# Overlapping the up-projection units of a gated feed-forward block by half, and taking their follow-up work one by one from a list

## The chip, the cores and the metric

The kernel runs on one core of a Trainium2 chip. The metric is device microseconds of one execution, the median of several runs. The core's engines run their own queues in order: TensorE (PE, with its weight loads as PEld), VectorE (DVE), ScalarE (ACT), GpSimd (POOL) and SyncE (SP), which here only issues transfers.

## What is computed

One layer of a streaming encoder over 2048 positions of width 1024: a mixer (pooling and a gated recurrence) and then the part that this change touches, a feed-forward block with a short convolution over the positions.

```python
def conv_glu_ffn(x, w_up, conv_w, conv_b, w_down):
    S = x.shape[1]
    h = x @ w_up                                   # 1024 -> 2 * 2816
    hp = jnp.pad(h, ((0, 0), (CONV_WIDTH - 1, 0), (0, 0)))
    hc = sum(conv_w[j] * hp[:, j:j + S] for j in range(CONV_WIDTH)) + conv_b
    val, gate = jnp.split(hc, 2, axis=-1)
    return (jax.nn.silu(gate) * val) @ w_down
...
        x = x + conv_glu_ffn(rmsnorm(x, norm2_g[l]), w_up[l], conv_w[l], conv_b[l], w_down[l])
```

All values are float32. D_FF is 2816, which is 22 tiles of 128.

## The kernel before, in words

The positions are worked off in two rounds of 1024, each round as two halves of 512 (hf 0 and 1): mixer, output projections, up-projection, down-projection. `ffn` (from line 1327) does the last two.

A **unit** m of the up-projection (m = 0 to 21) makes four results of 128 channels by 512 positions: the value and the gate (s = 0 and 1) of channel tile m, for both halves. It does so with seven products instead of eight (a Winograd scheme of 2 by 2 blocks, the blocks being the two halves of the 1024 inputs, value and gate, and the two halves of the positions). A product is a sum over four tiles of inputs, and since each float32 operand is split into a high and a low part, each tile takes three matmuls: twelve matmuls of 128 by 128 by 512 per product (`Unit.multiply`, line 146 being the helper's line for every matmul). The combinations of the positions ("forms", 56 tiles) are made once per round and stay in place; those of the weights are read from memory as raw tiles.

The products are added up in three PSUM banks per unit: P1 and P2 in X, P6, P7 and P4 in Z, P5 and P3 in V. Between them copies are taken (`Unit.after`): e1 is X after P1 (ScalarE, line 993), u2 is e1 - Z after P6 (VectorE, line 995), u3 is Z - e1 after P7 (line 999). P7 must wait for u2, since it adds to the bank that u2 reads; P4 must wait for u3, and P3 for the result h of the gate's second half (line 959), which reads V. The order within a unit is P1, P6, P5, P7, P2, P4, P3. P2 completes the value of half 0, P7 the gate of half 1, P4 the gate of half 0 (line 957), P3 the value of half 1.

The order of the units (`up_order`): units 0 and 1 alternate, then 2 and 3 (their first two products ahead of the rest), and from unit 4 on one unit follows the other whole.

What follows a result (`emit_up`): `conv` copies two halo columns (GpSimd, lines 1343 and 1345), takes the first tap on ScalarE (line 1348) and adds two taps on VectorE (lines 1350 and 1352); `glu` takes SiLU on ScalarE (line 1356) and multiplies gate and value on VectorE (lines 1358 and 1360; GpSimd does line 1360 for units 0 to 3). `add_forms` then makes the seven operands of the down-projection from the gated tiles of two neighbouring units: three are the tiles themselves, stored by SP (line 1334), and four are sums on GpSimd (line 1065), stored from its queue (line 1372). The down-projection (`Rows`, tiles dn_P) fetches them back (line 777) and splits them (lines 578 and 579).

Weights come as a stream: SP loads raw tiles (line 183, eight buffers), ScalarE makes the high part (line 205) and VectorE the low part (line 206) of an operand tile `ops`, of which there are six. So the cast for product j waits until product j - 6 has been done. Casts are placed at most four products ahead of the product that is being written.

The rest of the working tiles share one pool of 77 slots, of which the forms hold 56 during the up-projection. A new tile waits until its slot's last user is done, the store of a form among them.

The order on each engine comes from a scheduler that plays the program with durations of its own and puts instructions where they could start; a program line says what depends on what. `behind` forces one instruction behind another on the same engine, `in_turn` keeps an instruction from being placed ahead of the last matmul written so far. Neither makes a semaphore. In `ffn` the convolutions and gates of a result are written where the result is, all that are due at once; the sums of forms are written two products after their gate (`later`, `turn`, `FORM_LAG`), and the stores at the next product that is not P3 (`flush`).

Of the kernel before, what the change touches and what calls it, by code (L numbers as in the profile page):

```python
# [14 lines left out]
AF = mybir.ActivationFunctionType  # L15
ALU = mybir.AluOpType
# [11 lines left out]
MF = D_FF // P  # L28
EPS = 1e-6
TB = 512  # L30
# [19 lines left out]
ORDER = ("P1", "P6", "P5", "P7", "P2", "P4", "P3")  # L50
# [11 lines left out]
N_HEADS = 2  # L62
# [7 lines left out]
N_RAW = 8  # L70
GROUP = 4
SUM_LAG = 7
FORM_LAG = 2
N_OPS = 6
LOOKAHEAD = 4
MM_PER_TICK = 6
# [3 lines left out]
def tile_trunk(  # L80
# [16 lines left out]
    pe, act, dve, pool, sp = nc.tensor, nc.scalar, nc.vector, nc.gpsimd, nc.sync  # L97
# [9 lines left out]
    def slot(name, cols=TB, dt=F32):  # L107
        return slots.tile([P, cols], dt, tag="s", name=name, padded_shape=[P, 528])
# [121 lines left out]
    def behind(ins, other):  # L230

        tc.add_manual_dep(ins.ins, other.ins.name, mybir.DependencyInfo(
            mybir.DependencyClass.NoSync, mybir.DependencyReason.DATA), reason="behind")

    def in_turn(ins):

        tc.add_manual_dep(ins.ins, count[1].ins.name, mybir.DependencyInfo(
            mybir.DependencyClass.NoSync, mybir.DependencyReason.SCHED_ONLY), reason="in turn")
# [159 lines left out]
    def up_order():  # L398
        heads = [(0, 1), (2, 3), (4, 5)][:N_HEADS]
        res = [(m, p) for ms in heads for p in ("P1", "P2") for m in ms]  # L400
        res += [(m, p) for ms in heads for p in ("P6", "P5", "P7", "P4", "P3") for m in ms]
        return res + [(m, p) for m in range(2 * N_HEADS, MF) for p in ORDER]

    def plan_ffn():
        units = {}
        for m, p in up_order():
            if m not in units:
                units[m] = sums_of_unit(w_up_t, m, MF + m, sums["up"], m)
            fn, raws = units[m][p]()
            stream.op("up", fn, raws)  # L410
        plan_rows("dn", w_dn, R_DN, MF // 2)
# [91 lines left out]
    o_n1, o_n2, o_bg, o_ps, o_lb, o_hg, o_cb, o_cw = offs  # L503
# [8 lines left out]
    def col(o):  # L512
        return cols[:, o : o + 1]
# [97 lines left out]
    def norm_rows(src, name, xs, after, lag=1):  # L611
        for j in range(NT):
            while (src, j) not in ready:
                yield 1
            halves = [xt[src, j, c] for c in range(2)]
            t = [slot(f"{name}xs{j}_{hf}") for hf in range(2)]
            r = row_rstd(halves, t, f"{name}{j}")
            if lag:
                yield lag
            for hf in range(2):  # L620
                dve.tensor_scalar(t[hf], halves[hf], r[:, 0:1], None, ALU.mult)
                xs[j, hf] = t[hf]
            after(j)
# [327 lines left out]
    def value(dst, a, ps):  # L951
        if a is None:
            act.copy(dst, ps)
            return
        t, how = a
        if how == "from":
            dve.tensor_tensor(dst, ps, t, ALU.subtract)  # L957
        else:
            dve.tensor_tensor(dst, t, ps, ALU.add if how == "add" else ALU.subtract)  # L959

    class Unit:
# [28 lines left out]
        def after(self, p):  # L990
            bk, t = self.bank, self.t
            if p == "P1":
                act.copy(self.tmp("e1"), bk["X"])
            elif p == "P6":
                dve.tensor_tensor(self.tmp("u2"), t["e1"], bk["Z"], ALU.subtract)  # L995
            elif p == "P2":
                self.emit(0, 0, None, bk["X"])
            elif p == "P7":
                dve.tensor_tensor(self.tmp("u3"), bk["Z"], t["e1"], ALU.subtract)  # L999
                self.emit(1, 1, (t["u3"], "add"), bk["V"])  # L1000
            elif p == "P4":
                self.emit(1, 0, (t["e1"], "from"), bk["Z"])
            elif p == "P3":
                self.emit(0, 1, (t["u2"], "sub"), bk["V"])
# [54 lines left out]
    def add_forms(two, forms, k, name, store=lambda p, t: None, sums=True, pin=lambda i: None):  # L1059

        def comb(p, x0, x1, op):
            if (p, k) in forms or x0 is None or x1 is None:
                return
            t = slot(f"{name}_{p}_{k}")
            pin(pool.tensor_tensor(t, x0, x1, op))  # L1065
# [12 lines left out]
        comb("P3", forms.get(("P6", k)), two.get((1, 1)), ALU.add)  # L1078
# [247 lines left out]

    def ffn(b0, forms, late):
        gd, gt, gp = {}, {}, {}
        later, turn = [], [0]
        stores = []  # L1330

        def flush():
            for d, g in stores:
                sp.dma_start(d, g)
            stores.clear()

        def emit_up(m):
            hs, ts = {}, {}

            def conv(s, hf):  # L1340
                mt = m + MF * s
                h = hs[s, hf]
                pool.tensor_copy(h[:, 0:2], hist[:, mt] if hf == 0 else hs[s, 0][:, TB : TB + 2])  # L1343
                if hf == 1:
                    pool.tensor_copy(hist[:, mt], h[:, TB : TB + 2])  # L1345
                t = slot(f"e{b0}_{m}_{s}_{hf}")
                ts[s, hf] = t
                act.activation(t, h[:, 2:], AF.Identity, bias=col(o_cb + mt),  # L1348
                               scale=col(o_cw + 4 * MF + mt))
                dve.scalar_tensor_tensor(t, h[:, 1 : 1 + TB], col(o_cw + 2 * MF + mt), t,  # L1350
                                         ALU.mult, ALU.add)
                dve.scalar_tensor_tensor(t, h[:, 0:TB], col(o_cw + mt), t, ALU.mult, ALU.add)  # L1352

            def glu(hf):
                g = ts[1, hf]
                act.activation(g, g, AF.Silu)  # L1356
                if hf:
                    dve.scalar_tensor_tensor(g, g, -1.0, ts[0, hf], ALU.mult, ALU.mult)  # L1358
                else:
                    (pool if m < G_POOL else dve).tensor_tensor(g, g, ts[0, hf], ALU.mult)  # L1360
                k = m // 2
                two = gp.setdefault(k, {})
                two[hf, m % 2] = g

                def store(p, t):
                    name = f"dg{b0}_{p}_{k}"
                    d = dram.tile([P, TB], F32, tag=name, name=name)
                    gd[p, k] = d
                    if p in R_FORM:
                        stores.append((d, t))  # L1370
                    else:
                        pool.dma_start(d, t)  # L1372

                have = dict(two)
                add_forms(have, gt, k, f"gf{b0}", store, False)
                later.append((turn[0] + FORM_LAG, lambda: add_forms(
                    have, gt, k, f"gf{b0}", store, True, in_turn)))

            def emit(s, hf, a, ps):
                h = slot(f"h{b0}_{m}_{s}_{hf}", 2 + TB)  # L1380
                hs[s, hf] = h
                value(h[:, 2:], a, ps)
                first = (0, 0) if m >= 2 * N_HEADS else (1, 0)
                if (s, hf) == first:
                    conv(0, 0)
                if (s, hf) == (1, 0):
                    conv(1, 0)
                    glu(0)
                elif (s, hf) == (0, 1):
                    conv(0, 1)  # L1390
                    conv(1, 1)
                    glu(1)

            return emit

# [40 lines left out]
        for n, (m, p) in enumerate(up_order()):  # L1436
            if n == GO_AT:
                go_up[0] = True
            if m not in units:
                units[m] = Unit(f"up{b0}_{m}", "up", emit_up(m))  # L1440
            u = units[m]
            u.multiply(p, forms, late)
            turn[0] = n
            while later and later[0][0] <= n:
                later.pop(0)[1]()
            if p != "P3":
                flush()
            u.after(p)
            if m == MF - 1 and p in EARLY:
                down.make(EARLY[p])  # L1450

        for _, fn in later:
            fn()
        last = b0 + 2 >= SEQ // TB
        nxt = []

# [104 lines left out]
```

## Time and profile before

| | us |
|---|---|
| runs of the kernel | 2723.14, 2713.98, 2723.79 (median 2723.14) |
| the profiled execution | 2727.51, its span 2725.0 |
| mean granted TensorE clock of its span | 0.977 of full speed |
| up-projection, first round | 689.0 to 1165.4 |
| up-projection, second round | 2017.1 to 2495.7 |

Times in the profile count from the first instruction. Tile names are printed without numbers: up_X, up_Z and up_V are the three banks, up_e, up_u (both u2 and u3) and h the copies, e the convolved and gated tiles, gf_P the sums and dg_P their copies in memory, ops the weights' operand tiles, raw the loaded weights. The forms show the product in a matmul's name: m_f0 to m_f3 is P1, m_f4 to m_f7 P2, m_T1 P5, m_T2 P6, m_T3 P7, m_T4 P4, m_B22 P3; the letter h or l is the high or low part. In a row of the timeline stand start, duration, engine, line, operation, tiles, and in brackets the idle time before it and what ended that.

### The profile page before, as it was taken

The numbers are of one execution on the slowest core, as the hardware profiler recorded it, in microseconds if no ns is written. First come the engines' busy times: TensorE is split into PE (matmuls) and PEld (weight loads), VectorE is DVE, ScalarE is ACT, GpSimd is POOL, SyncE is SP. The second block draws the span as 40 slices with busy tenths as digits, with TensorE's granted clock in tenths as the row PEclk, the third lists the DMA queues.
The fourth block names the chain that finished last, engine by engine and source line by source line (L and its number), as shares of the span: only waits on it lengthen the run. The fifth ranks groups of instructions, "written<-read, shape, count | busy, mean of one in ns | idle before, by whom it ended". The sixth has DMA issues, their size and how long they took to land. (4 is left out here: it accounts for less than half of the span.)

```text
span 2725.0 us, 35432 instructions
## 1 busy us (share of the span) xinstructions
PE 2568.9 (94%) x11464; PEld 2077.4 (76%) x11464; DVE 1990.4 (73%) x3390; ACT 1166.1 (43%) x2204; POOL 963.7 (35%) x1273
## 2 busy tenths in 40 slices
PE   7899999889989999989989999999998899999998
PEld 6678887767767777768868788888786677777886
DVE  7888878358787777766577787675779777777744
ACT  5333434214544444444464344442355444444533
POOL 5544343061453343443253111201434323324402
PEclk8999999989989999999999999999999999999999
DMA  5656567889577788899888434346343443435942
GB/s 204 214 147 167 169 160 196 247 256 250 159 191 207 206 225 234 239 315 352 246 243 236 132 120 132 120 154 231 121 151 105 132 127 131 144 125 190 342 143 105
DMA packets 258313, 515.75 MB, mean 189 GB/s; under 512 B 26224, under 2 KB 42736, under 8 KB 257648
## 3 DMA queue, kind: packets, MB, share of 16 engines
q1 hardware_dynamic: 177600, 301.01, 34.1%
q0 software_dynamic: 51040, 129.52, 19.6%
q10 hardware_dynamic: 29488, 82.96, 8.6%
q8 instruction: 90, 1.47, 0.2%
q14 instruction: 95, 0.78, 0.1%
HBM read 422.69 MB, written 206.05 MB: 231 GB/s over the span
## 5 line engine op out<-in xcount | busy, mean ns | idle before, releaser
L205 ACT CAST ops<-raw 128x512 fp32r<-128x512 f32 x732 | 451.2, 620 | 932.6 <-PE up_Z L146 241.5
L206 DVE TENSOR_TENSOR ops<-raw,ops 128x512 fp32r<-128x512 f32 x732 | 563.4, 773 | 300.7 <-ACT ops L205 292.5
L1348 ACT ACTIVATE e<-h,cols 128x512 f32<-128x512 f32 x176 | 138.6, 813 | 19.3 <-DVE h L959 8.6
L1352 DVE SCALAR_TENSOR_TENSOR e<-h,cols,e 128x512 f32<-128x512 f32 x176 | 144.3, 825 | 0.0
L1065 POOL TENSOR_TENSOR gf_P<-e,e 128x512 f32<-128x512 f32 x44 | 77.8, 1769 | 171.8 <-DVE e L1358 113.0
L1350 DVE SCALAR_TENSOR_TENSOR e<-h,cols,e 128x512 f32<-128x512 f32 x176 | 134.6, 787 | 3.4
L777 POOL DMA_DIRECT2D g_P<-dg_P x154 | 86.2, 565 | 135.4 <-PE dn_P L146 49.5
L1343 POOL COPY h<-h 128x2 f32<-128x2 f32 x88 | 54.2, 642 | 152.8 <-DVE h L957 152.8
L1345 POOL COPY hist<-h 128x2 f32<-128x2 f32 x88 | 40.7, 462 | 180.3 <-DVE h L959 180.0
L146 PE MATMUL up_Z<-m_T30h,ops 128*128 128x512 f32 x88 | 39.6, 450 | 53.8 <-DVE up_u L995 53.8
L1276 POOL TENSOR_TENSOR ya<-ya,gl 128x512 f32<-128x512 f32 x32 | 46.2, 1473 | 112.0 <-DVE gl L1268 110.5
L999 DVE TENSOR_TENSOR up_u<-up_Z,up_e 128x512 f32<-128x512 f32 x44 | 30.4, 690 | 72.5 <-PE up_Z L146 72.4
L146 PEld LDWEIGHTS up_Z<-m_T30h,ops 128*128 128x128 f32 x88 | 17.2, 195 | 71.4 <-DVE up_u L995 38.1
L826 POOL COPY qm<-q 128x64 f32<-128x64 f32 x64 | 28.9, 462 | 118.2 <-DVE q L850 25.0
L1356 ACT ACTIVATE e<-e 128x512 f32<-128x512 f32 x88 | 54.9, 624 | 32.9 <-DVE e L1352 32.8
L1209 ACT ACTIVATE gt<-gt,cols 128x512 f32<-128x512 f32 x48 | 34.8, 725 | 78.8 <-DVE gt L959 61.3
L1172 POOL TENSOR_TENSOR q<-q,qs 128x512 f32<-128x512 f32 x16 | 21.9, 1371 | 127.4 <-ACT qs L1171 114.3
L1041 DVE TENSOR_TENSOR ac<-ac,dn_P 128x512 f32<-128x512 f32 x72 | 46.8, 682 | 27.7 <-PE dn_P L146 20.2
L959 DVE TENSOR_TENSOR h<-up_u,up_V 128x512 f32<-128x512 f32 x88 | 60.2, 684 | 5.4 <-PE up_V L146 3.9
L1065 POOL TENSOR_TENSOR gf_P<-gf_P,e 128x512 f32<-128x512 f32 x44 | 59.0, 1340 | 11.0 <-DVE e L1358 10.3
L1372 POOL DMA_DIRECT2D dg_P<-gf_P x88 | 55.6, 632 | 19.3 <-POOL gf_P L1065 18.7
L1041 DVE TENSOR_TENSOR x<-x,wo_P 128x512 f32<-128x512 f32 x88 | 56.1, 680 | 7.7 <-PE wo_P L146 7.6
(1270 smaller groups left out, 8367.7 us busy)
## 6 DMA issues: line engine op xcount, KB each, us to landing
g_P<-dg_P POOLq DMA_DIRECT2D x154, 256.0 KB, 7.1
raw<-in_w_up_t SPq DMA_DIRECT2D x132, 256.0 KB, 2.9
raw<-in_w_in_t SPq DMA_DIRECT2D x98, 256.0 KB, 2.9
dg_P<-gf_P POOLq DMA_DIRECT2D x88, 256.0 KB, 3.4
raw<-in_w_io SPq DMA_DIRECT2D x68, 256.0 KB, 5.2
dg_P<-e SPq DMA_DIRECT2D x66, 256.0 KB, 3.0
raw<-in_w_dn SPq DMA_DIRECT2D x66, 256.0 KB, 6.0
x<-in_x SPq DMA_DIRECT2D x64, 256.0 KB, 5.2
```

The costliest lines, as they stand in the source:

```text
L146: count[1] = pe.matmul(*args, **kw)
L205: self.mark = act.copy(hi, v)
L206: dve.tensor_tensor(lo, v, f32(hi), ALU.subtract)
L777: eng.dma_start(t, d)
L959: dve.tensor_tensor(dst, t, ps, ALU.add if how == "add" else ALU.subtract)
L1041: dve.tensor_tensor(t, t, ps[j], ALU.add if sg > 0 else ALU.subtract)
L1065: pin(pool.tensor_tensor(t, x0, x1, op))
L1348: act.activation(t, h[:, 2:], AF.Identity, bias=col(o_cb + mt), scale=col(o_cw + 4 * MF + mt))
L1350: dve.scalar_tensor_tensor(t, h[:, 1 : 1 + TB], col(o_cw + 2 * MF + mt), t, ALU.mult, ALU.add)
L1352: dve.scalar_tensor_tensor(t, h[:, 0:TB], col(o_cw + mt), t, ALU.mult, ALU.add)
L1356: act.activation(g, g, AF.Silu)
L1372: pool.dma_start(d, t)
```

## The change

From unit 4 on the products of unit m are given the places 7m, 7m + 2, ... 7m + 12, and sorted. So two neighbouring units alternate, half a unit apart: P7 of unit m, P1 of m+1, P2 of m, P6 of m+1, P4 of m, P5 of m+1, P3 of m, P7 of m+1, and so on.

The convolutions, gates and sums of forms are no longer written where the result is, but put on a list, `work`; after each product one entry of it is written (`drain(1)`; sums of forms cost nothing and are written as soon as they stand first). A unit adds six entries and has seven products, and units 0 to 3 add six each too, mostly at once. The taps on ScalarE and SiLU are kept `in_turn`, and the first VectorE tap of a convolution is also put `behind` the newest u2 or u3. What was still on the list is written after the last product. The stores are issued after every product, P3 as well. The number of instructions does not change.

```diff
-        return res + [(m, p) for m in range(2 * N_HEADS, MF) for p in ORDER]
+
+        rest = [(7 * m + 2 * i, m, p) for m in range(2 * N_HEADS, MF)
+                for i, p in enumerate(ORDER)]
+        return res + [(m, p) for _, m, p in sorted(rest)]
...
+    def first(ins):
+
+        urgent[0] = ins
+
+    def second(ins):
+        if urgent[0] is not None:
+            behind(ins, urgent[0])
+        return ins
...
-                dve.tensor_tensor(self.tmp("u2"), t["e1"], bk["Z"], ALU.subtract)
+                first(dve.tensor_tensor(self.tmp("u2"), t["e1"], bk["Z"], ALU.subtract))
...
-                dve.tensor_tensor(self.tmp("u3"), bk["Z"], t["e1"], ALU.subtract)
+                first(dve.tensor_tensor(self.tmp("u3"), bk["Z"], t["e1"], ALU.subtract))
...
+        def drain(n):
+            while work and (n or not work[0][0]):
+                k, fn = work.pop(0)
+                n -= k
+                fn()
...
-                act.activation(t, h[:, 2:], AF.Identity, bias=col(o_cb + mt),
-                               scale=col(o_cw + 4 * MF + mt))
-                dve.scalar_tensor_tensor(t, h[:, 1 : 1 + TB], col(o_cw + 2 * MF + mt), t,
-                                         ALU.mult, ALU.add)
+                in_turn(act.activation(t, h[:, 2:], AF.Identity, bias=col(o_cb + mt),
+                                       scale=col(o_cw + 4 * MF + mt)))
+                in_turn(second(dve.scalar_tensor_tensor(t, h[:, 1 : 1 + TB],
+                                                        col(o_cw + 2 * MF + mt), t,
+                                                        ALU.mult, ALU.add)))
...
-                act.activation(g, g, AF.Silu)
+                in_turn(act.activation(g, g, AF.Silu))
...
-                later.append((turn[0] + FORM_LAG, lambda: add_forms(
-                    have, gt, k, f"gf{b0}", store, True, in_turn)))
+                work.append((0, lambda: add_forms(have, gt, k, f"gf{b0}", store, True, in_turn)))
...
                 if (s, hf) == first:
-                    conv(0, 0)
+                    work.append((1, lambda: conv(0, 0)))
                 if (s, hf) == (1, 0):
-                    conv(1, 0)
-                    glu(0)
+                    work.append((1, lambda: conv(1, 0)))
+                    work.append((1, lambda: glu(0)))
                 elif (s, hf) == (0, 1):
-                    conv(0, 1)
-                    conv(1, 1)
-                    glu(1)
+                    work.append((1, lambda: conv(0, 1)))
+                    work.append((1, lambda: conv(1, 1)))
+                    work.append((1, lambda: glu(1)))
...
             u.multiply(p, forms, late)
-            turn[0] = n
-            while later and later[0][0] <= n:
-                later.pop(0)[1]()
-            if p != "P3":
-                flush()
+            flush()
             u.after(p)
+            drain(1)
...
-        for _, fn in later:
-            fn()
+        while work:
+            drain(1)
```

What it moves is shown by the orders of the two programs. First VectorE where units follow one another: the twelve rows around u2 of unit 9 in the first round. In `up0_9_u2` the 0 is the round and 9 the unit; in `e0_8_0_1` stand round, unit, s and half; ops and raw carry the number of the product. Before:

```order
L206 TENSOR_TENSOR ops239_8206<-raw225_8009,ops239_8206 128x512
L1350 SCALAR_TENSOR_TENSOR e0_8_0_1_8165<-h0_8_0_1_8161,cols_84,e0_8_0_1_8165 128x512
L1350 SCALAR_TENSOR_TENSOR e0_8_1_1_8171<-h0_8_1_1_8091,cols_84,e0_8_1_1_8171 128x512
L1352 SCALAR_TENSOR_TENSOR e0_8_0_1_8165<-h0_8_0_1_8161,cols_84,e0_8_0_1_8165 128x512
L1360 TENSOR_TENSOR e0_8_1_0_8137<-e0_8_1_0_8137,e0_8_0_0_8113 128x512
L1352 SCALAR_TENSOR_TENSOR e0_8_1_1_8171<-h0_8_1_1_8091,cols_84,e0_8_1_1_8171 128x512
L206 TENSOR_TENSOR ops240_8230<-raw226_8039,ops240_8230 128x512
L206 TENSOR_TENSOR ops241_8247<-raw227_8063,ops241_8247 128x512
L1358 SCALAR_TENSOR_TENSOR e0_8_1_1_8171<-e0_8_1_1_8171,e0_8_0_1_8165 128x512
L995 TENSOR_TENSOR up0_9_u2_8221<-up0_9_e1_8197,up0_9_Z_8199 128x512
L206 TENSOR_TENSOR ops242_8273<-raw228_8080,ops242_8273 128x512
L999 TENSOR_TENSOR up0_9_u3_8263<-up0_9_Z_8199,up0_9_e1_8197 128x512
```

Now (the line numbers are those of the changed program, u2 being line 1008, u3 1012, the taps 1369 and 1372, the gate 1378, the cast 205):

```order
L1012 TENSOR_TENSOR up0_8_u3_8061<-up0_8_Z_7944,up0_8_e1_7911 128x512
L205 TENSOR_TENSOR ops236_8103<-raw222_7903,ops236_8103 128x512
L972 TENSOR_TENSOR h0_8_1_1_8063<-up0_8_u3_8061,up0_8_V_7997 128x512
L1369 SCALAR_TENSOR_TENSOR e0_7_0_1_8067<-h0_7_0_1_8037,cols_84,e0_7_0_1_8067 128x512
L1372 SCALAR_TENSOR_TENSOR e0_7_0_1_8067<-h0_7_0_1_8037,cols_84,e0_7_0_1_8067 128x512
L1369 SCALAR_TENSOR_TENSOR e0_7_1_1_8093<-h0_7_1_1_7885,cols_84,e0_7_1_1_8093 128x512
L205 TENSOR_TENSOR ops237_8134<-raw223_7928,ops237_8134 128x512
L1372 SCALAR_TENSOR_TENSOR e0_7_1_1_8093<-h0_7_1_1_7885,cols_84,e0_7_1_1_8093 128x512
L205 TENSOR_TENSOR ops238_8164<-raw224_7954,ops238_8164 128x512
L1378 SCALAR_TENSOR_TENSOR e0_7_1_1_8093<-e0_7_1_1_8093,e0_7_0_1_8067 128x512
L1008 TENSOR_TENSOR up0_9_u2_8147<-up0_9_e1_8089,up0_9_Z_8127 128x512
L205 TENSOR_TENSOR ops239_8189<-raw225_7977,ops239_8189 128x512
```

u2 of unit 9 stood behind cast 241 and the gate of unit 8, with two casts and two convolutions of unit 8 close before it; it now stands behind cast 238 and the gate of unit 7. Its P6 is product 235 before and 233 now.

Second, VectorE around u2 of unit 4, the first that used to run alone. Before:

```order
L206 TENSOR_TENSOR ops206_7377<-raw192_7149,ops206_7377 128x512
L1350 SCALAR_TENSOR_TENSOR e0_3_0_1_7285<-h0_3_0_1_7281,cols_84,e0_3_0_1_7285 128x512
L1350 SCALAR_TENSOR_TENSOR e0_3_1_1_7291<-h0_3_1_1_7159,cols_84,e0_3_1_1_7291 128x512
L1352 SCALAR_TENSOR_TENSOR e0_3_0_1_7285<-h0_3_0_1_7281,cols_84,e0_3_0_1_7285 128x512
L1352 SCALAR_TENSOR_TENSOR e0_3_1_1_7291<-h0_3_1_1_7159,cols_84,e0_3_1_1_7291 128x512
L206 TENSOR_TENSOR ops207_7399<-raw193_7170,ops207_7399 128x512
L1358 SCALAR_TENSOR_TENSOR e0_3_1_1_7291<-e0_3_1_1_7291,e0_3_0_1_7285 128x512
L995 TENSOR_TENSOR up0_4_u2_7351<-up0_4_e1_7327,up0_4_Z_7329 128x512
L999 TENSOR_TENSOR up0_4_u3_7389<-up0_4_Z_7329,up0_4_e1_7327 128x512
```

Now:

```order
L205 TENSOR_TENSOR ops204_7274<-raw190_7069,ops204_7274 128x512
L1369 SCALAR_TENSOR_TENSOR e0_2_1_0_7241<-h0_2_1_0_7153,cols_84,e0_2_1_0_7241 128x512
L1372 SCALAR_TENSOR_TENSOR e0_2_1_0_7241<-h0_2_1_0_7153,cols_84,e0_2_1_0_7241 128x512
L205 TENSOR_TENSOR ops205_7299<-raw191_7092,ops205_7299 128x512
L1008 TENSOR_TENSOR up0_4_u2_7285<-up0_4_e1_7263,up0_4_Z_7267 128x512
L205 TENSOR_TENSOR ops206_7321<-raw192_7116,ops206_7321 128x512
L1369 SCALAR_TENSOR_TENSOR e0_3_0_0_7288<-h0_3_0_0_6693,cols_84,e0_3_0_0_7288 128x512
L1369 SCALAR_TENSOR_TENSOR e0_3_1_0_7311<-h0_3_1_0_7178,cols_84,e0_3_1_0_7311 128x512
L1372 SCALAR_TENSOR_TENSOR e0_3_0_0_7288<-h0_3_0_0_6693,cols_84,e0_3_0_0_7288 128x512
```

Before, all convolutions and gates of units 2 and 3 stood ahead of it. Now the second half of unit 2 and all of unit 3 follow it: it is row 1080 of VectorE's order and was row 1096.

More of the change, by code (lines that the diff above doesn't have):

```diff
@@ L72 @@
 SUM_LAG = 7
-FORM_LAG = 2
 N_OPS = 6
@@ L233, in behind @@
             mybir.DependencyClass.NoSync, mybir.DependencyReason.DATA), reason="behind")
+    urgent = [None]
+    def first(ins):
[4 more added lines that the diff above has]
+        return ins
     def in_turn(ins):
@@ L1328, in ffn @@
         gd, gt, gp = {}, {}, {}
-        later, turn = [], [0]
+        work = []
         stores = []
```

## The prediction

> **What bounds the kernel now.** I read the busy shares first, then the list of who waited for whom on TensorE, then windows around the two up-projection stages, then the timeline of TensorE, VectorE and GpSimd inside a stage. The page's first part says who is full, and the waits say what little stops it (columns: total us, times, longest).
>
> ```profile
> PE 2568.9 (94%) x11464; PEld 2077.4 (76%) x11464; DVE 1990.4 (73%) x3390; ACT 1166.1 (43%) x2204; POOL 963.7 (35%) x1273
> ```
> ```profile
> PE up_Z L146 <- DVE up_u L995: 53.8, 20, 8.3
> PE x_t L627 <- DVE x_xs L621: 10.1, 4, 7.7
> PE dn_P L146 <- ACT dn_P_10h L578: 7.4, 1, 7.4
> ```
>
> TensorE is busy for 94% of the span, and no other engine is near that. The one wait of size is in the stage that the change touches: 53.8 us in 20 pieces, each time a product into bank Z waiting for VectorE's `up_u`, the copy (u2) that must be taken out of Z before the next product is added to it. The windows give the two rounds, each split into units 0 to 3 and units 4 to 21 (first column after the stretch: its length; then busy us of PE, PEld, DVE, ACT, POOL, clock, DMA share, GB/s).
>
> ```profile
> 689.00:783.30 94.30, 86.83 (x369) 67.92 (x368) 78.61 (x109) 49.44 (x87) 45.33 (x52) 0.96 0.65 171
> 783.30:1165.40 382.10, 358.95 (x1514) 285.74 (x1514) 290.53 (x403) 173.43 (x275) 148.22 (x209) 0.98 0.80 223
> 2017.00:2111.10 94.10, 86.78 (x370) 67.91 (x369) 79.67 (x109) 49.56 (x88) 39.88 (x48) 0.96 0.34 107
> 2111.10:2495.70 384.60, 359.90 (x1514) 286.79 (x1514) 292.58 (x403) 172.81 (x276) 127.10 (x191) 0.98 0.42 136
> ```
>
> The timeline of TensorE gives the price of one product of twelve matmuls, and shows the hole.
>
> ```profile
> 874.63 0.40 PE L146 MATMUL up_V<-m_B223h,ops 128*128 128x512 f32 x1
> 877.41 0.39 PE L146 MATMUL up_X<-m_f3h,ops 128*128 128x512 f32 x1
> 880.20 0.40 PE L146 MATMUL up_Z<-m_T23h,ops 128*128 128x512 f32 x1
> ...
> 882.99 0.39 PE L146 MATMUL up_V<-m_T13h,ops 128*128 128x512 f32 x1
> 885.42 0.50 PE L146 MATMUL up_Z<-m_T30h,ops 128*128 128x512 f32 x1 [2.05 <-DVE up_u L995]
> ```
> ```profile
> 904.79 0.39 PE L146 MATMUL up_V<-m_T13h,ops 128*128 128x512 f32 x1
> 905.20 0.47 PE L146 MATMUL up_Z<-m_T30h,ops 128*128 128x512 f32 x1
> ```
>
> The first three rows are the last matmuls of P3, P1 and P6: 874.63, 877.41, 880.20, so 2.78 us a product without a wait. P5 ends with the row at 882.99; P7 should start 0.23 us later and starts 2.43 us later, at 885.42. One unit later it starts 0.41 us late (904.79 to 905.20). A large hole in every second unit is the pattern. The queue in front of u2 says why.
>
> ```profile
> 881.29 1.29 DVE L206 TENSOR_TENSOR ops<-raw,ops 128x512 fp32r<-128x512 f32 x1 [0.42 <-ACT ops L205]
> 882.50 2.27 DVE L1358 SCALAR_TENSOR_TENSOR e<-e,e 128x512 f32<-128x512 f32 x1
> 884.69 0.67 DVE L995 TENSOR_TENSOR up_u<-up_e,up_Z 128x512 f32<-128x512 f32 x1
> ```
> ```profile
> 882.92 1.29 POOL L1065 TENSOR_TENSOR gf_P<-gf_P,e 128x512 f32<-128x512 f32 x1
> 885.10 1.29 POOL L1065 TENSOR_TENSOR gf_P<-gf_P,e 128x512 f32<-128x512 f32 x1
> ```
> ```profile
> 903.09 0.69 DVE L206 TENSOR_TENSOR ops<-raw,ops 128x512 fp32r<-128x512 f32 x1 [0.42 <-ACT ops L205]
> 903.76 0.69 DVE L1358 SCALAR_TENSOR_TENSOR e<-e,e 128x512 f32<-128x512 f32 x1
> ```
>
> P6 ended near 880.4, but u2 (884.69) stands behind a weight cast and the gate of the unit before (L1358), which took 2.27 us while GpSimd ran form sums (odd units have three of them) and 0.69 us a unit later without. Between P6 and P7 lies only P5, 2.78 us, so a u2 that ends 5.0 us after P6 stops TensorE.
>
> **Part by part.**
>
> *Alternating products.* Eighteen units of seven products at 2.78 us are 350.3 us. The windows have 382.1 and 384.6: an excess of 31.8 and 34.3, together **66.1 us**, and all of it is holes at P7 and their clock loss. In the new order unit m's P6 is followed by the neighbour's P4, its own P5 and the neighbour's P3 before its own P7: u2 gets 8.34 us instead of 2.78. u3 (read after P7, before P4) gets the same instead of 2.78, and the value copied from V before P3 gets five products instead of two. The steady lateness of 5.0 us is covered with 3.3 to spare. The cover is VectorE's order as well: u2 must not stand behind work that needs a later product. Number the products as their weight tiles are numbered (ops235 belongs to product 235): a cast j waits, through its ring of six operand buffers, for product j-6. Before, u2 of unit 9 stood behind cast 241, which needs product 235, the same P6 that u2 waits for. Now its P6 is product 233, and it stands behind cast 238, which needs product 232, the one before. If the cover went, each unit would pay what it pays now.
>
> VectorE must also hold the rate.
>
> ```profile
> 940.00:1020.00 80.00, 77.46 (x332) 61.69 (x331) 60.36 (x87) 37.56 (x60) 33.09 (x46) 1.00 0.80 208
> ```
>
> 332 matmuls of 84 are 3.95 units, so VectorE is busy 60.36 / 3.95 = 15.3 us a unit, GpSimd 8.4 and ScalarE 9.5. The unit shrinks from 20.3 to 19.5 us: VectorE fills 79% of it. No engine is full, so the excess can go.
>
> *Unit 4.* It starts alone (P1, P6, P5, P7 in a row), so its u2 keeps 2.78 us, and its hole is the largest.
>
> ```profile
> 791.46 0.39 PE L146 MATMUL up_V<-m_T13h,ops 128*128 128x512 f32 x1
> 800.16 0.77 PE L146 MATMUL up_Z<-m_T30h,ops 128*128 128x512 f32 x1 [8.31 <-DVE up_u L995]
> 800.72 0.63 PE L146 MATMUL up_Z<-m_T30l,ops 128*128 128x512 f32 x1
> 801.15 0.63 PE L146 MATMUL up_Z<-m_T30h,ops 128*128 128x512 f32 x1
> ```
> ```profile
> 799.33 0.68 DVE L995 TENSOR_TENSOR up_u<-up_e,up_Z 128x512 f32<-128x512 f32 x1
> ```
>
> P6's last matmul started one product before the row at 791.46, so at 788.7, and u2 ends at 800.0, 11 us after it. Behind the hole the matmuls come 0.43 us apart (800.72 to 801.15) instead of 0.23: the clock was halved, and that loss is part of the excess. The list takes convolutions of units 2 and 3 one product at a time, and puts them behind u2: counted from u2 of unit 0, which is row 1004 in both orders, u2 of unit 4 is row 1080 instead of 1096. Sixteen instructions at about 0.69 us are 11 us earlier, just enough. I leave 1.5 us a round of the excess: **-3** (bounds 0 and 2 x 8.3).
>
> *Units 0 to 3.* Their products keep their order; only VectorE's queue changes.
>
> ```profile
> 764.41 0.39 PE L146 MATMUL up_Z<-m_T33h,ops 128*128 128x512 f32 x1
> 767.88 0.76 PE L146 MATMUL up_Z<-m_T30h,ops 128*128 128x512 f32 x1 [3.08 <-DVE up_u L995]
> ```
> ```profile
> 2093.88 0.39 PE L146 MATMUL up_Z<-m_T33h,ops 128*128 128x512 f32 x1
> 2097.19 0.47 PE L146 MATMUL up_Z<-m_T30h,ops 128*128 128x512 f32 x1 [2.92 <-DVE up_u L995]
> ```
>
> Unit 3's u2 stands 12 rows earlier (1049 instead of 1061), some 8 us, so both 3 us holes should close: **+6** (0 to 8; minus 6 if the spread convolutions make a new one at a P4).
>
> *The list itself, and the order pins.* They add no instruction and no semaphore. What waits longer is the convolutions: they run up to six products later at units 4 and 5 and hold their tiles for longer. A tile that has to be stored before its slot is free can stop an engine; the nearest row is this wait of ScalarE, and I charge one per round, **-4.8** (0 to 20).
>
> ```profile
> ACT ops L205 <- DMA dg_P<-e: 2.4, 1, 2.4
> ```
>
> *Form sums right behind the gate.* Without the lag, GpSimd's sums (1.29 us) and the small halo copies that the next convolution needs come in another order; a halo copy can wait for two sums and a store issue, under 4 us, and with it a VectorE tap and the u2 behind it. That is inside the 8.34 us: nothing. SP's stores are issued after every product; weights are loaded eight tiles ahead, which hides that: nothing.
>
> *Down-projection behind it.* In the first round DMA is full there.
>
> ```profile
> 1185.00:1205.00 20.00, 20.00 (x88) 16.18 (x88) 10.61 (x19) 6.45 (x12) 9.03 (x16) 1.00 1.03 334
> ```
> ```profile
> PE dn_P L146 <- ACT dn_P_6h L578: 5.9, 1, 5.9
> ```
>
> The fetches that end this 5.9 us wait come through full queues; if up-projection ends 35 us earlier, part of what it loaded beside its holes moves here: **-3** (0 to 32, the first round's whole gain). The second round has a DMA share of 0.42 and nothing to give back.
>
> *Sum.* 66.1 - 3 + 6 - 4.8 - 3 = 61 us. The profiled execution took 2727.5 us (span 2725.0): 2666. It is 4.4 us above the median of the runs shown (2723.1; they lie from 2714.0 to 2723.8), so on the scale of the median I forecast **2662 us**.
>
> **Rivals.**
>
> *DMA takes the first round's gain back* in down-projection: 34.3 + 3 stay, 2723 - 37 = 2686. For it: the share of 1.03. Against: over the whole of up-projection the share is 0.80, and TensorE stood still only 5.9 us there.
>
> *The reorder does half:* VectorE comes out of units 0 to 3 late, with 109 instructions in 94 us and 78.6 busy, and its backlog moves along, so that P7, or the P4 behind u3, waits on in many units. Half of 66 is 33: 2690. Against: 4.2 us a unit are free to work a backlog off.
>
> *VectorE becomes the bound, slower.* The form sums now fall among the convolutions. The row first: L1358 took 2.27 instead of 0.69 us beside a GpSimd sum. The Trainium skill, "SBUF — State Buffer", section "Who interferes with whom", says that a VectorE instruction with two SBUF inputs and a GpSimd instruction that reads SBUF exclude each other for the whole instruction; the trace agrees, with 2.27 us beside sums of 1.29. By that rule any sum placed beside a convolution costs VectorE its whole length. From the rows: VectorE's 15.3 us a unit may grow by at most GpSimd's 8.4. Up to 4.2 the unit stays at 19.5; from 5.0 on it is longer than today's 20.3; at three quarters (6.3) it is 21.6, 1.3 us more in 36 units, +47: 2770. Against: the same sums run today, and they are in the 15.3 already.
>
> *No change:* the hole moves to another wait of the same size, a tile slot or a store; 2723. For it: many more tiles are alive. Against: nothing in the order waits for a store that is less than four products old.
>
> **How the numbers follow.** Forecast 0.72; DMA 0.10; half 0.08; no change 0.06; VectorE bound 0.04. The range reaches from all excess and both early holes gone (2723 - 74, and 4 us of spread: 2645) to a little past the half case (2695). A difference of 0.5%, 13.6 us, is about what a measurement of this kernel can tell from no change. Faster by more: 0.90; within: 0.06; slower: 0.04.
>
> **What would show it.** Right: the wait of up_Z for up_u falls from 53.8 us to under 10; the windows of units 4 to 21 last 351 to 356 us at a clock of 1.00; in the timeline u2 (now L1008) ends before P5 does, two products ahead of its P7. Wrong: new rows "PE up_Z" or "PE up_V" behind u3 (now L1012) or h; GpSimd or ScalarE rows waiting for dg_P stores; longer dn_P waits in the first round alone (DMA); VectorE busy above 18 us a unit.

## The result, and the profile after

| | before | after |
|---|---|---|
| median of 4 runs, us | 2723.47 (2713.98 to 2724.79) | 2649.18 (2647.05 to 2653.14) |
| ratio, 95% interval | | 0.9736 (0.9711 to 0.9761) |
| profiled execution, us (span) | 2727.51 (2725.0) | 2647.05 (2645.3) |
| up-projection, both rounds, us | 955.0 | 878.1 |
| everything else in the span, us | 1770.0 | 1767.2 |

The forecast was 2662 us with 2645 to 2695. Nearly the whole gain is in the two up-projection stages: 76.9 of the 79.7 us by which the spans differ. (The medians differ by 74.3: the profiled execution of before is 4.0 us above its median, that of after 2.1 below.)

The busy shares of the changed kernel:

```profile
PE 2534.1 (96%) x11464; PEld 2057.6 (78%) x11464; DVE 1965.5 (74%) x3390; ACT 1169.8 (44%) x2204; POOL 942.2 (36%) x1273
```

The top of TensorE's list of waits (total us, times, longest):

```profile
PE x_t L640 <- DVE x_xs L634: 9.5, 3, 7.7
PE dn_P L145 <- ACT dn_P_10h L591: 7.2, 1, 7.2
PE dn_P L145 <- ACT dn_P_6h L591: 6.8, 1, 6.8
```

The row that led the list before, 53.8 us of up_Z behind `up_u`, has gone from it, and nothing has come in its place: these three stood there before with 10.1, 7.4 and 5.9. The windows over units 0 to 3 and 4 to 21 of each round (length; busy us of PE, PEld, DVE, ACT, POOL; clock, DMA share, GB/s):

```profile
682.27:770.84 88.57, 83.80 (x370) 65.82 (x368) 72.89 (x102) 47.07 (x83) 38.41 (x48) 1.00 0.61 163
770.84:1121.85 351.01, 351.01 (x1514) 284.13 (x1513) 290.69 (x409) 177.13 (x278) 145.27 (x214) 1.00 0.91 247
1979.40:2067.85 88.45, 83.69 (x369) 65.82 (x368) 72.92 (x103) 46.98 (x83) 34.83 (x44) 1.00 0.34 101
2067.85:2417.92 350.07, 350.07 (x1514) 284.03 (x1513) 288.74 (x408) 177.07 (x279) 121.85 (x194) 1.00 0.50 152
```

In units 4 to 21 TensorE's busy time equals the length of the window, at full clock. 351.0 and 350.1 us are within 0.7 us of the 350.3 us of eighteen units without any wait. VectorE does the same work as before there (290.7 against 290.5 us). Around one P7, first TensorE (the last matmul of a unit's P6, the last of its P5, the first of its P7), then VectorE:

```profile
868.05 0.39 PE L145 MATMUL up_Z<-m_T23h,ops 128*128 128x512 f32 x1
...
873.62 0.39 PE L145 MATMUL up_V<-m_T13h,ops 128*128 128x512 f32 x1
...
876.62 0.39 PE L145 MATMUL up_Z<-m_T30h,ops 128*128 128x512 f32 x1
```
```profile
867.68 0.69 DVE L1378 SCALAR_TENSOR_TENSOR e<-e,e 128x512 f32<-128x512 f32 x1
868.48 0.69 DVE L1008 TENSOR_TENSOR up_u<-up_e,up_Z 128x512 f32<-128x512 f32 x1
```

The gate is done when P6 ends, and u2 follows at once. It is finished at 869.2, 7.4 us before P7 adds to its bank. So u2 is not late and then covered; it isn't late at all. Here it ends 0.9 us after P6 (counted from 0.23 us after the start of its last matmul, when the next one starts); over units 5 to 21 of both rounds it is 0.9 to 2.1 us, where before it was 2.7 to 5.0. That raises the question of what the distance between P6 and P7 is for, and the experiments take it up.

### The profile page after: what moved, and what is told of

It reads as the page before. It is cut to its first block, busy times and chain, and to the rows that moved or that the text cites. A ratio compares the mean times of both kernels' runs of the same rounds, so it can differ in the third digit from the quotient of the medians.

```text
span 2645.3 us, 35486 instructions
## 1 busy us (share of the span) xinstructions
PE 2534.1 (96%) x11464; PEld 2057.6 (78%) x11464; DVE 1965.5 (74%) x3390; ACT 1169.8 (44%) x2204; POOL 942.2 (36%) x1273
## 5 line engine op out<-in xcount | busy, mean ns | idle before, releaser
L205 DVE TENSOR_TENSOR ops<-raw,ops 128x512 fp32r<-128x512 f32 x732 | 556.0, 763 | 241.6 <-ACT ops L204 234.4
L1078 POOL TENSOR_TENSOR gf_P<-e,e 128x512 f32<-128x512 f32 x44 | 67.7, 1541 | 150.0 <-DVE e L1378 96.8
L1362 POOL COPY h<-h 128x2 f32<-128x2 f32 x88 | 40.3, 476 | 115.6 <-DVE h L970 113.7
L847 PE MATMUL pl<-qm,k 128*128 128x192 f32 x256 | 48.5, 332 | 6.6 <-DVE qm L843 3.0
L847 PEld LDWEIGHTS pl<-qm,k 128*128 128x128 f32 x256 | 43.3, 192 | 11.1 <-ACT ops L204 4.1
L1006 ACT COPY up_e<-up_X 128x512 f32<-128x512 f32 x44 | 25.8, 586 | 56.9 <-PE up_X L145 51.9
```

Source lines behind the costliest of these rows:

```text
L205: dve.tensor_tensor(lo, v, f32(hi), ALU.subtract)
L847: pe.matmul(pa_[:, c * 192 : c * 192 + 192], ks[:, (i + c) * P : (i + c + 1) * P], mv[:, c].rearrange("p s x -> p (s x)"), start=True, sto ...
```

## The experiments

The theory on record names two things: where u2 stands in VectorE's queue, and how far P7 stands from P6. The profile of before shows a third, the gate that took 2.27 us beside GpSimd's sums. The rivals are that one of the three does everything. All kernels below ran beside the kernel before; its median was 2721 us for both groups of four. The stages' lengths are from the windows of each profiled execution, both rounds added; 18 units without waits are 2 x 350.3 = 700.6.

| kernel | median us | ratio to before (95%) | units 4-21 | units 0-3 |
|---|---|---|---|---|
| before | 2721 | 1 | 766.6 | 188.4 |
| changed | 2649.2 | 0.9736 (0.9711-0.9761) | 701.1 | 177.0 |
| order of products alone | 2676.8 | 0.9835 (0.9819-0.9852) | 721.3 | 187.6 |
| list alone | 2664.0 | 0.9796 (0.9773-0.9818) | 709.7 | 180.7 |
| before, sums 5 products late | 2657.2 | 0.9765 (0.9750-0.9779) | 706.6 | 180.7 |
| before, short sums | 2666.3 | 0.9800 (0.9785-0.9815) | 723.0 | 179.9 |
| before, sums not late | 2764.8 | 1.0153 (1.0127-1.0179) | 791.6 | 199.5 |
| changed, sums doubled | 2659.1 | 0.9782 (0.9755-0.9808) | 706.0 | 179.3 |
| list alone, sums doubled | 2731.4 | 1.0040 (1.0022-1.0058) | 778.1 | 176.9 |
| order, sums 5 products late | 2662.2 | 0.9782 (0.9763-0.9801) | 705.8 | 182.9 |

Outside the two stages the profiled executions took 1764 to 1784 us. The two highest, list alone and changed with sums doubled, are of executions that were 10 and 11 us above the median of their kernel, so a row's stages and its median can differ by that much.

**The order of products alone** (the kernel before with the new `up_order`):

```diff
-        return res + [(m, p) for m in range(2 * N_HEADS, MF) for p in ORDER]
+        rest = [(7 * m + 2 * i, m, p) for m in range(2 * N_HEADS, MF)
+                for i, p in enumerate(ORDER)]
+        return res + [(m, p) for _, m, p in sorted(rest)]
```

> The kernel before with the new order of products alone; convolutions and gates are still written where the result is, the sums two products later. In VectorE's order u2 of units 5 to 21 now stands behind the cast that needs the product before its P6, as in the changed kernel, and P7 comes four places after P6 instead of two. Unit 4's u2 still stands behind all convolutions of units 2 and 3 (row 1096 as before), and units 0 to 3 are as before. Theory A (the gain comes from u2's place in the queue and its distance to P7): the holes of units 5 to 21 go, unit 4 (8.3 us and its clock loss, 10 us a round) and units 0 to 3 (94 us a round) stay: 65.6 - 20 = 46 us, 2677. Rival B (the list does it, the order of products nothing): the bulk convolutions keep u2 late, 2715 or more. Rival C (the order of products alone does all): unit 4 heals too, 2650.

2676.8 us, theory A's number. What is left of the wait, and its largest piece, unit 4's in the first round:

```profile
PE up_Z L146 <- DVE up_u L998: 21.5, 4, 7.8
```
```profile
790.76 0.39 PE L146 MATMUL up_V<-m_T13h,ops 128*128 128x512 f32 x1
798.94 0.77 PE L146 MATMUL up_Z<-m_T30h,ops 128*128 128x512 f32 x1 [7.79 <-DVE up_u L998]
```

The wait is in four pieces now instead of 20, at units 3 and 4 of each round, and unit 4 still pays a hole of 7.8 us and a stretch of half clock behind it (the matmuls that follow are 0.43 us apart). The regular holes are gone. So the list is what mends units 3 and 4, and it isn't needed for the rest. But this order moves the sums too: the 44 gates of this kernel have a mean of 689 ns instead of 1259. The new order of products alone thus takes away all three, the place, the short distance and the slow gate, and doesn't tell them apart.

**The list alone** (the changed kernel with the old order of products):

```diff
-        rest = [(7 * m + 2 * i, m, p) for m in range(2 * N_HEADS, MF)
-                for i, p in enumerate(ORDER)]
-        return res + [(m, p) for _, m, p in sorted(rest)]
+        return res + [(m, p) for m in range(2 * N_HEADS, MF) for p in ORDER]
```

> The changed kernel with the old order of products: one unit after another, but convolutions, gates and sums taken one by one from the list. u2 of every unit now stands behind the cast that needs the product before its P6, and its gate comes later; P7 still follows P6 with only P5, 2.78 us, between. Theory A1 (u2's place in VectorE's queue is what counts; 2.78 us are enough for one copy of 0.7 us): holes gone everywhere, within 0.5% of the changed kernel, 2645 to 2660. Rival A2 (the distance of 8.34 us is what counts): u2 is still late whenever a GpSimd sum stretches the row ahead of it, a hole in every second unit stays, half of the gain: 2685 to 2700. Rival: the list costs more than it gives without the alternation, 2723 or above.

2664.0 us, 0.6% above the changed kernel and 4 us past A1's range: nearer to A1 than to A2. Only three P7 a round are still late by more than 0.2 us, those of units 6, 7 and 9; unit 6 in VectorE's order:

```profile
825.11 1.77 DVE L1366 SCALAR_TENSOR_TENSOR e<-h,cols,e 128x512 f32<-128x512 f32 x1
826.81 1.94 DVE L205 TENSOR_TENSOR ops<-raw,ops 128x512 fp32r<-128x512 f32 x1
828.68 0.74 DVE L1369 SCALAR_TENSOR_TENSOR e<-h,cols,e 128x512 f32<-128x512 f32 x1
829.34 0.67 DVE L1005 TENSOR_TENSOR up_u<-up_e,up_Z 128x512 f32<-128x512 f32 x1
```

A tap of 1.77 and a cast of 1.94 us, instead of 0.75 and 0.69, put u2 behind its time. A place ahead of the cast that needs P6 is nearly enough with 2.78 us of distance, but every stretched row is felt.

**The sums five products late** (the kernel before, one number):

```diff
-FORM_LAG = 2
+FORM_LAG = 5
```

> The kernel before with one number changed: the sums of forms are written five products after their gate instead of two. The scheduler then also places u2 of units 4 to 21 ahead of the gate and behind the cast that needs the product before P6; the order of products is unchanged. A1 (place in the queue): nearly the whole gain, 2650 to 2670. A2 (distance between P6 and P7): no change, 2715 to 2727. Port theory (only the sums beside the gate matter): the large holes of every second unit go, units 4 and 0 to 3 partly, 2680 to 2695.

2657.2 us, as A1 said: 64 of the 74 us with the order of products and the bulk writing as they were. The scheduler puts the gate behind u2. The groups of its profile (busy us, mean ns) and the neighbourhood of a late sum, VectorE and TensorE:

```profile
L1358 DVE SCALAR_TENSOR_TENSOR e<-e,e 128x512 f32<-128x512 f32 x44 | 55.8, 1268 | 0.2
```
```profile
857.30 0.68 DVE L995 TENSOR_TENSOR up_u<-up_e,up_Z 128x512 f32<-128x512 f32 x1
857.90 1.19 DVE L206 TENSOR_TENSOR ops<-raw,ops 128x512 fp32r<-128x512 f32 x1
859.01 2.31 DVE L1358 SCALAR_TENSOR_TENSOR e<-e,e 128x512 f32<-128x512 f32 x1
```
```profile
859.50 0.39 PE L146 MATMUL up_V<-m_T13h,ops 128*128 128x512 f32 x1
859.73 0.39 PE L146 MATMUL up_Z<-m_T30h,ops 128*128 128x512 f32 x1
```

The gates are as slow as before (before's group has 55.4 us and a mean of 1259 ns), this one 2.31 us, and P7 starts 0.23 us after P5's last matmul. A slow gate costs nothing if u2 stands ahead of it. In units 6 to 21 of both rounds u2 ends 1.0 us after P6.

**Short sums** (the kernel before):

```diff
-            pin(pool.tensor_tensor(t, x0, x1, op))
+            if name.startswith("gf"):
+                pin(pool.tensor_tensor(t[:, 0:64], x0[:, 0:64], x1[:, 0:64], op))
+                t = x0
+            else:
+                pin(pool.tensor_tensor(t, x0, x1, op))
```

> The kernel before with the sums of the down-projection's forms on GpSimd cut to 64 of 512 columns, and the first operand stored in the sum's place (the sums are left out of the result). VectorE's order in the up-projection is that of before up to the last unit, so u2 stands behind the same cast and the same gate. Port theory (GpSimd's sums stretch the gate from 0.69 to 2.27 us, and that makes the 2 us hole of every second unit): the holes of the odd units fall to the 0.4 us of the even ones, some 2.2 us with the clock loss in 9 units a round: -40, 2683; the gate's row is 0.7 us everywhere. Queue theory alone (u2 behind a cast and a gate is late whatever the gate lasts): -0 to -10, 2713 to 2723, with the same holes.

2666.3 us, more than the 40 us expected: units 4 to 21 gave 43.6, and units 0 to 3, which the expectation left out, 8.5. (The large holes of before are those of the even units, whose u2 stands behind the gate of an odd one; the expectations of this run and of the next read as if they were the odd units'.) The kernel leaves the sums out of its result and stores an operand in their place. The place of u2 is the same as before, and the gate is short; here in unit 8, whose P7 waited 2.05 us before:

```profile
L1362 DVE SCALAR_TENSOR_TENSOR e<-e,e 128x512 f32<-128x512 f32 x44 | 30.2, 686 | 0.4
```
```profile
867.47 0.69 DVE L206 TENSOR_TENSOR ops<-raw,ops 128x512 fp32r<-128x512 f32 x1 [0.42 <-ACT ops L205]
868.08 0.68 DVE L1362 SCALAR_TENSOR_TENSOR e<-e,e 128x512 f32<-128x512 f32 x1
868.68 0.68 DVE L995 TENSOR_TENSOR up_u<-up_e,up_Z 128x512 f32<-128x512 f32 x1
```
```profile
774.95:1136.77 361.82, 356.73 (x1514) 284.69 (x1513) 263.52 (x401) 171.56 (x274) 114.05 (x211) 0.99 0.85 236
```

```profile
PE up_Z L146 <- DVE up_u L995: 11.7, 4, 5.5
```

Cast, gate and u2, 0.69, 0.68 and 0.68 us, just fit between P6 and P7: in units 5 to 21 u2 ends 2.7 to 2.8 us after P6, and P7 comes 0.34 to 0.41 us after P5's last matmul instead of 0.23. The last row is what is left of the wait: four pieces, at units 3 and 4 of each round, of at most 5.5 us where it was 8.3. So the sums were the cause of the regular hole as much as the place in the queue was. VectorE is busy 263.5 us instead of 290.5: the full sums cost it 27 us a round.

**The sums not late** (the kernel before):

```diff
-FORM_LAG = 2
+FORM_LAG = 0
```

> The kernel before with the sums of forms written right behind their gate (lag 0 instead of 2). In VectorE's order u2 of the even units now stands behind a cast that needs P5, the product after its P6, and five rows; u2 of the odd units stands as before, behind the cast that needs P6 and the gate. By the place in the queue: u2 of an even unit cannot end before P5 has ended plus three rows of 0.7 us, so the 2 us holes are now in the even units whatever the sums do, and units 2 to 4 are worse (ten to twelve rows): 2715 to 2745. By the sums alone (they no longer lie beside the gate that u2 stands behind): the holes go, 2665 to 2690.

2764.8 us: the direction that the place in the queue gives, 20 us beyond its range; by the sums alone it should have come down to 2665 to 2690. Units 4 to 21 lost 25.0 us and units 0 to 3 11.1. The gates are all short, yet a hole stands in every even unit, as before, and a longer one; here unit 10:

```profile
L1358 DVE SCALAR_TENSOR_TENSOR e<-e,e 128x512 f32<-128x512 f32 x44 | 30.3, 689 | 4.1 <-ACT e L1356 2.1
```
```profile
927.10 0.69 DVE L206 TENSOR_TENSOR ops<-raw,ops 128x512 fp32r<-128x512 f32 x1
927.88 0.69 DVE L1358 SCALAR_TENSOR_TENSOR e<-e,e 128x512 f32<-128x512 f32 x1
928.49 0.68 DVE L995 TENSOR_TENSOR up_u<-up_e,up_Z 128x512 f32<-128x512 f32 x1
```
```profile
926.00 0.39 PE L146 MATMUL up_V<-m_T13h,ops 128*128 128x512 f32 x1
929.23 0.50 PE L146 MATMUL up_Z<-m_T30h,ops 128*128 128x512 f32 x1 [2.84 <-DVE up_u L995]
```

The cast of 927.10 needs P5, whose last matmul started at 926.00, and u2 stands behind it and the gate; P7 waits 2.84 us. Stretched rows are not needed for a hole: a bad place makes one with short rows.

**The sums doubled**, in the changed kernel and in the list alone:

```diff
-            pin(pool.tensor_tensor(t, x0, x1, op))
+            for _ in range(2 if name.startswith("gf") else 1):
+                pin(pool.tensor_tensor(t, x0, x1, op))
```

> The changed kernel with every sum of the down-projection's forms made twice on GpSimd: 88 more sums of some 1.3 to 1.5 us. Theory (8.34 us between P6 and P7 absorb any row that a sum stretches): no hole at P7, units 4 to 21 stay at 351 to 355 us a round, 2645 to 2660, VectorE's busy time up by 20 to 80 us. Rival (VectorE becomes the bound, the slower case of the prediction): units grow beyond 19.5 us, +40 or more, 2690 and above.

> The same doubling on the list with the old order of products, where P7 follows P6 after one product, 2.78 us. If the distance is what absorbs a stretched row: holes of 1 to 3 us come back at P7 in every second unit, 20 to 40 us above the list alone (2664): 2685 to 2705. If u2's place in the queue is all that counts: within 0.5% of the list alone, 2651 to 2677.

2659.1 and 2731.4 us. The same load costs the changed kernel 10 us and the list alone 67, which is more than expected and brings it back to before. The changed kernel's first round of units 4 to 21 with doubled sums, and the wait at the head of up_Z's in the list alone with them:

```profile
779.06:1134.31 355.25, 351.82 (x1514) 283.78 (x1513) 321.53 (x409) 169.75 (x278) 210.16 (x254) 1.00 0.88 244
```
```profile
PE up_Z L145 <- DVE up_u L1005: 33.8, 13, 5.2
```

VectorE is busy for 321.5 of 355.3 us in the first, and the stretch is only 4.2 us longer than in the changed kernel. One of the holes of the second, on VectorE and on TensorE:

```profile
891.18 1.94 DVE L205 TENSOR_TENSOR ops<-raw,ops 128x512 fp32r<-128x512 f32 x1
893.04 2.02 DVE L1367 SCALAR_TENSOR_TENSOR e<-h,cols,e 128x512 f32<-128x512 f32 x1
895.09 2.12 DVE L1370 SCALAR_TENSOR_TENSOR e<-h,cols,e 128x512 f32<-128x512 f32 x1
897.14 1.74 DVE L1367 SCALAR_TENSOR_TENSOR e<-h,cols,e 128x512 f32<-128x512 f32 x1
898.81 0.67 DVE L1005 TENSOR_TENSOR up_u<-up_e,up_Z 128x512 f32<-128x512 f32 x1
```
```profile
893.99 0.39 PE L145 MATMUL up_V<-m_T13h,ops 128*128 128x512 f32 x1
899.63 0.76 PE L145 MATMUL up_Z<-m_T30h,ops 128*128 128x512 f32 x1 [5.25 <-DVE up_u L1005]
```

Four rows in a line are stretched to about 2 us, and u2 ends 8.0 us after P6; P7 is due 2.78 us after P6 and waits. In the changed kernel with the same load u2 is as late, and P7 is not. Unit 7 of its first round: P6's last matmul, u2, and P7's first:

```profile
839.99 0.39 PE L145 MATMUL up_Z<-m_T23h,ops 128*128 128x512 f32 x1
848.57 0.39 PE L145 MATMUL up_Z<-m_T30h,ops 128*128 128x512 f32 x1
```
```profile
846.12 0.68 DVE L1008 TENSOR_TENSOR up_u<-up_e,up_Z 128x512 f32<-128x512 f32 x1
```

u2 ends at 846.8, 6.6 us after P6, and P7 starts when it would have started anyway, 8.34 us after P6. In 23 of the 34 units 5 to 21 of both rounds u2 ends more than 2.78 us after P6, at most 8.6 us, and in the worst of them P7 comes 0.4 us late. This is what the distance is for: it doesn't make the gain, it keeps it, and here it is nearly used up.

**Order and late sums without the list** (the two small edits of above together):

> The kernel before with the new order of products and the sums written five products after their gate, without the list. Both causes are then removed in units 5 to 21, and u2 of unit 4 stands ahead of the gate. If this is all that the list brings: 2645 to 2657, the changed kernel's time. If the list is needed for unit 4 and units 2 and 3: the remainder seen with lag 5 alone, some 9 us in the two stages, stays: 2655 to 2665.

2662.2 us, the second case. The stages are 10.6 us longer than the changed kernel's, of which 3.2 are the clock at P6 of units 0 and 1 (below), 4.4 are unit 4's late P7 (its P5 takes 4.75 and 5.25 us to the next product instead of 2.78), and 3.4 lie at P7 of units 2 and 3 (7.45 and 7.13 us for the two, against 5.60 and 5.54); 0.7 came back behind P6. Two small edits don't replace the list; no variant beat the changed kernel, whose units 4 to 21 have nothing left to win without a shorter product.

The pin that puts a convolution's first tap `behind` the newest u2 or u3 had no run of its own: the program built without it has the same order on every engine, row for row.

## Why the prediction held, step by step

**The excess of 66.1 us.** Units 4 to 21 gave 65.5. The split is as put: the order of products alone takes 45.3 of it (766.6 to 721.3), the list the rest at unit 4. The step that failed is the reason given first, that u2's lateness of 5.0 us is covered by 8.34. In the changed kernel u2 is 0.9 to 2.1 us behind P6, so the lateness was removed rather than covered: u2 stands ahead of the cast that needs its P6, and the gates are mostly short (a mean of 767 ns instead of 1259). The old distance of 2.78 us would have done for that. The prediction had that place only as a condition ("The cover is VectorE's order as well"); it did the work. A regular hole of before took three things at once: u2 behind the cast of its own P6, a slow row ahead of it, and one product of distance. That the first or the second ends it is shown one at a time (the place by late sums, where the gates stay slow; the slow row by short sums, where the place stays). A worse place makes a hole without a slow row (sums not late). The order of products alone takes away all three at once. The distance by itself is shown only against doubled sums, where u2 ends up to 8 us after P6 in both orders and only the longer distance keeps P7 on time; what it alone would do to the kernel before has no run.

**Unit 4, -3.** Nothing was left of its hole, which is 2.4 us more than the sum had for units 4 to 21. With the list alone it is gone too, in both rounds.

**Units 0 to 3, +6.** 11.4 us. The holes at unit 3's P7 gave 8.0 with their clock (P7 of units 2 and 3 together took 10.43 and 8.72 us before, 5.60 and 5.54 after), the upper bound of the term. Another 4.1 came at P6 of units 0 and 1, where both kernels have the same products and the same waits, and 0.7 of them went again at the next product. That is luck, not the change: see the last section.

**Slot waits, -4.8.** ScalarE's own waits for stores went from 2.4 us in one piece to 3.1 in four, none over 0.8, and TensorE lost nothing to them; the charge was wrong. **Down-projection, -3.** The wait on dn_P_6h grew from 5.9 to 6.8, so 0.9 us, and outside the stages 2.8 us were gained where 3 were charged. (The prediction reads 5.9 us as all of TensorE's standstill there; it leaves out a second wait of the same stage, on dn_P_10h, 7.4 us before and 7.2 after.) The DMA share in units 4 to 21 rose from 0.80 to 0.91 and from 0.42 to 0.50 and gave nothing back, which ends that rival. Together 2.4, 5.4, 4.8 and 5.8 us are the 18.4 us by which the gain of the profiled executions, 79.7, exceeded the sum, 61.3 before rounding. So the middle of the forecast was 13 us too high, and the pieces all erred to the same side, among them two charges that did not come (10.6 us) and 3.4 us of luck.

**VectorE as the bound.** It didn't happen: same busy time. But the mechanism is real, and a shorter distance meets it: see the doubled sums. The Trainium skill, "SBUF — State Buffer", section "Who interferes with whom", says that a VectorE instruction with two SBUF inputs and a GpSimd instruction that reads SBUF shut each other out, and that one with at most one SBUF input is not concerned. The traces agree on both: gates, casts and taps went from 0.7 to 2.3 us beside one sum, and with the sums doubled a tap took 5.57 us beside four sums in a row, while u2, with one input in PSUM, has group means of 677 to 686 ns in all ten kernels. The rival's guess that three quarters of GpSimd's time would come back as VectorE's was high: doubling the sums added 64.9 us to GpSimd in the first round's units 4 to 21 and 30.8 to VectorE, about half.

## What to carry to other kernels

When an engine waits for a short instruction of another, look at the rows ahead of that instruction on its own queue: one that needs the same event, or one that a third engine can stretch, is a hole waiting to open. Cure it by the place in the queue first (here one number, the lag of unrelated sums, moved it and gave 64 of 74 us), and buy distance as insurance against rows that stretch. Test a margin by doubling the load it is meant for: two kernels that were 0.6% apart were 2.7% apart under it.

## What the runs showed of the hardware

The same gap doesn't always cost the same. At P6 of unit 0, where all kernels have the same products, TensorE waits 1.84 and 0.75 us for forms. In the changed kernel and in the kernel before, first round:

```profile
712.50 0.50 PE L145 MATMUL up_Z<-m_T23h,ops 128*128 128x512 f32 x1 [1.84 <-ACT m_T23h L591]
713.75 0.50 PE L145 MATMUL up_Z<-m_T23l,ops 128*128 128x512 f32 x1 [0.75 <-DVE m_T23l L592]
714.09 0.40 PE L145 MATMUL up_Z<-m_T23h,ops 128*128 128x512 f32 x1
714.32 0.39 PE L145 MATMUL up_Z<-m_T20h,ops 128*128 128x512 f32 x1
```
```profile
719.25 0.51 PE L146 MATMUL up_Z<-m_T23h,ops 128*128 128x512 f32 x1 [1.84 <-ACT m_T23h L578]
720.50 0.80 PE L146 MATMUL up_Z<-m_T23l,ops 128*128 128x512 f32 x1 [0.75 <-DVE m_T23l L579]
721.10 0.63 PE L146 MATMUL up_Z<-m_T23h,ops 128*128 128x512 f32 x1
721.52 0.63 PE L146 MATMUL up_Z<-m_T20h,ops 128*128 128x512 f32 x1
```

After the same two waits the matmuls come 0.23 us apart in one and 0.43 in the other. Over the ten profiled kernels and two rounds this piece took 8.9 us nine times and 10.2 to 11.7 us eleven times, so 1.3 to 2.8 us of any comparison of single profiles are luck at this one place (0.4 of that comes back at the next product).

What decides is where the waits fall. In the records of the granted clock, in all ten traces, it changes only at points 3.413 us apart, to within 3 ns, and where these points lie against the first instruction differs from trace to trace. Take the time in which no matmul was started in the last 0.23 us as standstill, and add it up between one such point and the next. In the nine cases without loss the worst interval has 1.69 to 1.97 us of standstill, in the eleven with loss 2.03 to 2.81. It is the same in the whole of up-projection: of 2565 intervals at full clock 47 are followed by one at half clock, and all of these have 1.98 us of standstill or more, while no interval with more than 2.01 is followed by a full one. So a wait of 2 us costs its own length, or that and a stretch of half clock, by where it falls: the large regular holes of before, of 2.05 us, brought the half clock in 3 of 15. The Trainium skill, "TensorE: Matmul & The Clock Gate", Part 1, section "What's actually happening", puts the fall to half rate after at least one idle window of some 3.4 us and says that the window runs freely. The length of the window agrees with the 3.413 us here; but it need not be idle from end to end, 2.0 us of it were enough.

A GpSimd sum beside VectorE's gates is dear on both sides: GpSimd's sums of two gated tiles have a mean of 1331 ns in the kernel whose gates stay at 689 ns (sums not late) and 1933 ns in the one whose gates have 1268 (sums five products late).
